# A mixture-of-experts stage on one core: expert loads in a fixed order, the last splits in twos behind y, the low part of the tokens between the halves of the one-hot matrix

## The chip, the core and the metric

The kernel runs on one core of a Trainium2 chip. The core has a matrix engine (TensorE, PE in the rows; PEld is its weight load), VectorE (DVE), ScalarE (ACT), GpSimd (POOL) and SyncE (SP), which issues nearly all DMAs. The metric is the device time of one execution in microseconds, the median of the runs shown. A profile of one execution gives the trace from which all rows come.

## What is computed

Two blocks of a language model run one after the other on 256 tokens of width 1024, in float32. The first has two layers of windowed attention and a gated recurrence. The second has attention, a short convolution and, at its end, a mixture of experts. All of it stays as it is but for the last part:

```
h2 = rms_norm_2(x, ffn_norm_g)
x = x + hierarchical_moe(h2, ...)   # top-1 of 4 groups, top-2 of its 4 experts, gates normalised
#   per expert: hid = silu(h w_gate) * (h w_up) * combine;  out += hid w_down      (16 experts, 1024 -> 256 -> 1024)
h3 = rms_norm_2(x, ple_norm_g)
x = x + sigmoid(h3 w_pg) * (p w_ple)
```

## The kernel before, in words

Every instruction is written in a program order with a priority, and a list scheduler puts each engine's instructions into one fixed order when the kernel is built; on the chip each engine goes through its own list and waits on semaphores. `ahead(g, n)` shifts the priority, `tc.issue_after(x)` holds what is traced within it behind x on x's engine. Tiles of one tag share a number of buffers, and an instruction that needs a buffer waits for the one that frees it.

*Weights.* All weights lie in one tensor `w_all`, cut into units of 128 x 2048 float32 (1.05 MB). For most of the kernel `Stream.load` brings a unit into one of three `raw` buffers and `Stream.prepare` splits each half of it into a high and a low part: a cast on ACT (whi, L270) and a subtraction on DVE (wlo, L271), each into a tile of the pool `t4` (4 KB per partition, `g.nt4` = 24 of them). `mm3` (L363 to L365) then makes three matmuls for each product. The 48 expert units (`plain0` to `plain1`) are not split. `Stream.fetch(ahead)` loads them up to `ahead` units past the one in use: every fourth into a `raw` buffer, the others in two halves into t4 tiles (named `wx`). `refill` is called after each use and tops this up to 12 units; once all are issued, it begins on the last four units (tag "pg") and prepares as many halves as the tiles set free allow.

*Routing and gather.* `moe` handles the tokens as two tiles t of 128. `choose(t)` finds the experts on DVE and builds the one-hot matrix D (128 tokens x 16 experts x 64 places) in two halves (L1325). `parts(t)` then splits the normed tokens into hh (ACT, L1331) and hl (DVE, L1332), held behind the second half of D. `gather(i, k, t, j)` (L1390) multiplies tokens with D into places, for the experts 8i to 8i + 7, and copies the result into hs; i = 0 runs before the experts and i = 1 after the first pair's gate and up products. `to_slots` finds the largest count of tokens in an expert (cnt), puts the gates in the order of places (psc, L1416; cs) and transposes D into DT (L1426, L1427).

*Experts.* They go in eight pairs q. `gate_up(q, j)` (L1440, two units each), `product(q)` (silu on ACT L1447, product on DVE L1448), `turn(q)` (transposes L1454, hidT on ACT L1456), `down(q)` (L1467, two units) whose result y is split into yh (ACT) and yl (DVE) by `split_to` (L538), and `scatter(q, t)` (L1479), which adds y back to the tokens through DT into four accumulators. After the first pair stands `overflow` (L1519), a branch around code for experts with over 64 tokens; the instructions of its two sides can't be moved past it.

*End.* `ple_out` calls `finish(t, c)`, which for c = 0 scatters the last pair, and adds the accumulator to x (L1487). Then follow the norm weight (L1585), transposes (L1588), the split into h3, the squares for the norm, and the pg product in column halves with the tanh (L1610), the products (L1611, L1612) and the store (L1613).

The loop over the pairs, on which the order depends:

```
for q in range(NP):
    if q + 1 < NP: gate_up(q + 1, 0)
    turn(q)
    if q + 1 < NP: gate_up(q + 1, 1); product(q + 1)
    if q: scatter(q - 1, 0); scatter(q - 1, 1)
    down(q)
```

Of the kernel before, what the change touches and what calls it, by code (L numbers as in the profile page):

```python
# [9 lines left out]
F32 = mybir.dt.float32  # L10
# [169 lines left out]
class Stream:  # L180
    RAW = 3

    def __init__(self, g):
# [12 lines left out]
        self.pieces = {}  # L196

    def fetch(self, ahead):


        g = self.g
        while self.loaded < min(self.used + ahead, self.plain1):
            i = self.loaded
# [3 lines left out]
            if (i - self.plain0) % 4 == 0:  # L207
                t = g.wp.tile([128, 2080], F32, tag="raw", name="raw", bufs=3)
                g.nc.sync.dma_start(out=t[:, :w], in_=src)
                self.pieces[i] = t[:, :h], t[:, h:w]  # L210
            else:
# [3 lines left out]
            self.loaded += 1  # L215

    def plain(self, tag, n):
# [3 lines left out]
        self.fetch(1)  # L221
# [3 lines left out]
    def refill(self):  # L225

        self.fetch(12)
        k = self.used + 12 - self.plain1
        if self.loaded >= self.plain1 and k > 0:
# [3 lines left out]
            first = (self.plain1 - 12 - self.plain0) % 4  # L233
            raws = len([j for j in range(k) if (j + first) % 4 == 0])
            self.RAW = min(3, raws)
            self.prepare(min(2 * self.plain1 + k - raws, 2 * self.plain1 + 2 * raws))
# [989 lines left out]
def moe(g, last):  # L1226
# [49 lines left out]
    for t in range(2):  # L1276
# [3 lines left out]
        D.append(small(f"D{t}", (NE, CAP), F32R))  # L1280
# [15 lines left out]
    def choose(t):  # L1296
# [18 lines left out]
        nc.vector.scalar_tensor_tensor(sel[:, t], rank[:, t], 2.0, oh[:, t].unsqueeze(2).to_broadcast([128, 4, 4]),  # L1315
# [7 lines left out]
        for i in range(2):  # L1323
            e = slice(8 * i, 8 * i + 8)
            last = nc.vector.tensor_tensor(D[t][:, e], place[:, t, e].unsqueeze(2).to_broadcast([128, 8, CAP]),  # L1325
                                           g.c("iota").unsqueeze(1).to_broadcast([128, 8, CAP]), op=OP.is_equal)
        return last

    def parts(t, a, b):
        with tc.issue_after(a.ins), tc.issue_after(b.ins):  # L1330
            nc.scalar.activation(hh[t], xw[t], AF.Copy, scale=rs[t])  # L1331
            nc.vector.scalar_tensor_tensor(hl[t], xw[t], rs[t], hh[t].bitcast(F32), op0=OP.mult, op1=OP.subtract)  # L1332
# [26 lines left out]
    def end(t, moved):  # L1359
        rs.append(mr[t].end())  # L1360
        placed = choose(t)
        parts(t, moved, placed)
        combine(t)

    with ahead(g, -20):
# [8 lines left out]
        g.st.fetch(8)  # L1374
        end(1, begin(1, 1))
    fl.all()
    g.st.fetch(11)
# [24 lines left out]
    g.st.fetch(12)  # L1402

    cs = small("cs", (NP,))
    DT = small("DT", (NP, 256), F32R)

    def to_slots():
# [13 lines left out]
        for t in range(2):  # L1421
            for b in range(2):
                ps = g.sm.tile([128, 4, 128], F32, tag="s", name="DTp")
                for q in range(4):
                    o = (4 * b + q) * 128
                    nc.tensor.transpose(ps[:, q], slots[t][:, o:o + 128].bitcast(F32), g.c("ident"))  # L1426
                nc.scalar.copy(DT[:, 4 * b:4 * b + 4, t * 128:(t + 1) * 128], ps)  # L1427

# [3 lines left out]
    def gate_up(q, j):  # L1432
# [3 lines left out]
        for k in range(4):  # L1436
            kk = 4 * j + k
            for i in range(2):
                half, o = divmod(2 * q + i, 8)
                nc.tensor.matmul(hid[q][64 * i:64 * i + 64], hs[half][kk // 4][:, kk % 4, o * 64:(o + 1) * 64],  # L1440
                                 w[i][k // 2][:, k % 2], start=(kk == 0), stop=(kk == KT - 1), skip_group_check=True)
        g.st.refill()

# [14 lines left out]
    def down(q):  # L1458
# [3 lines left out]
        for c in range(2):  # L1462
# [6 lines left out]
            split_to(g, y[q][0][:, c2], y[q][1][:, c2], ps)  # L1469
        g.st.refill()  # L1470

    def scatter(q, t):
# [3 lines left out]
        for c in range(2):  # L1476
# [5 lines left out]
    def finish(t, c):  # L1482

        if c == 0:
            scatter(NP - 1, t)
# [4 lines left out]
    to_slots()  # L1490
    gate_up(0, 0)
    gate_up(0, 1)
    product(0)
    for k in range(KT):
        for t, j in ((0, 0), (0, 1), (1, 0), (1, 1)):
            gather(1, k, t, j)
    overflow(g, cnti, wb, rs, place, comb)
    g.wb = load_row(g, "wb", h["ple_norm_g_2"][0])
    for q in range(NP):
# [6 lines left out]
        if q:  # L1506
            for t in range(2):
# [65 lines left out]
def ple_out(g, out, finish):  # L1573
# [4 lines left out]
    for t in range(2):  # L1578
        ts = slice(t * 128, (t + 1) * 128)
        xw = t4(g, "xw3", shape=(128, DM))  # L1580
        with ahead(g, 100):
            for b in range(2):
# [6 lines left out]
                split_to(g, hT[0][:, 4 * b:4 * b + 4, ts], hT[1][:, 4 * b:4 * b + 4, ts], ps)  # L1589
# [59 lines left out]
```

## Time and profile before

| what | value |
|---|---|
| timed runs | 776.31 us median of 3 (773.83, 776.31, 778.20) |
| profiled execution | 773.34 us, span 771.5 us |
| PE busy | 751.2 us (97%) |
| DVE, ACT busy | 453.3 us (59%), 350.6 us (45%) |
| DMA | 153.31 MB, mean 199 GB/s |

The span runs from the first to the last instruction; the execution's own time holds a little more around it. Busy PE time is not PE at its peak, since matmuls overlap and their ends are modelled. The rows below give times from the start of the span. In rows of the timeline, a note in brackets is the idle time of the engine before the instruction, and what ended it.

### The profile page before, as it was taken

The page shows a single profiled execution, that of the slowest core. Times are in us where ns is not written, and L with a number is a line of the kernel's source. Part 1 is how long each engine was busy: PE and PEld are TensorE (multiplying, and loading weights), DVE is VectorE, ACT ScalarE, POOL GpSimd, SP SyncE. Part 2 cuts the span into 40 slices and gives each one's busy share as a digit, 9 for nine tenths or more (in the row PEclk, how much of TensorE's full clock was granted, in tenths as well). Part 3 has the DMA queues.
Part 4 walks back from the last instruction along what each step waited for, and adds up shares of the span by engine and source line. Part 5 has one row for each costly group of instructions (what it writes and reads, how often), then busy time and mean ns, then how long its engine had stood idle before and what let it go on. Part 6 is the DMA issues. An engine that isn't in the chain of part 4 may idle for free. (4 is left out here: it accounts for less than half of the span.)

```text
span 771.5 us, 11965 instructions
## 1 busy us (share of the span) xinstructions
PE 751.2 (97%) x4894; PEld 616.2 (80%) x4894; DVE 453.3 (59%) x731; ACT 350.6 (45%) x579; POOL 21.3 (3%) x33
## 2 busy tenths in 40 slices
PE   7999999999999999999999999999999999999787
PEld 5899899799789888979987889999998853333356
DVE  6687487757577836668588676955474421011472
ACT  6761345845466315656447566643533421010441
POOL 0000000000000001000001310000000000000000
PEclk9999999999999999999999999999999999999999
DMA  8873044375266403337535441566468469999801
GB/s 305 321 277 110 8 157 165 115 266 183 79 208 262 170 1 110 110 110 273 219 132 197 165 164 59 202 223 218 177 231 302 165 220 388 415 418 415 349 4 54
DMA packets 29883, 153.31 MB, mean 199 GB/s; under 512 B 4600, under 2 KB 5632, under 8 KB 16768
## 3 DMA queue, kind: packets, MB, share of 16 engines
q1 hardware_dynamic: 29680, 152.45, 53.1%
q8 instruction: 39, 0.64, 0.3%
q14 instruction: 20, 0.16, 0.1%
q10 hardware_dynamic: 144, 0.07, 0.0%
HBM read 151.45 MB, written 1.05 MB: 198 GB/s over the span
## 5 line engine op out<-in xcount | busy, mean ns | idle before, releaser
L271 DVE TENSOR_TENSOR wlo<-raw,whi 128x1024 fp32r<-128x1024 f32 (+1 forms) x182 | 217.3, 1221 | 75.6 <-ACT whi L270 72.7
L270 ACT CAST whi<-raw 128x1024 fp32r<-128x1024 f32 (+1 forms) x182 | 184.3, 1050 | 52.0 <-PE acc L364 29.9
L363 PE MATMUL acc<-hTh,whi 128*128 128x256 f32 x608 | 173.6, 286 | 0.0
L365 PE MATMUL acc<-hTh,wlo 128*128 128x256 f32 x608 | 171.9, 283 | 0.0
L364 PE MATMUL acc<-hTl,whi 128*128 128x256 f32 x608 | 171.7, 282 | 0.0
L365 PEld LDWEIGHTS acc<-hTh,wlo 128*128 128x128 f32 x608 | 114.7, 189 | 3.2 <-issue 3.2
L363 PEld LDWEIGHTS acc<-hTh,whi 128*128 128x128 f32 x608 | 114.6, 188 | 1.7 <-issue 1.2
L364 PEld LDWEIGHTS acc<-hTl,whi 128*128 128x128 f32 x608 | 114.7, 189 | 0.3 <-issue 0.2
L363 PE MATMUL acc<-whi,hTh 128*128 128x512 f32 (+2 forms) x224 | 84.9, 379 | 0.8 <-ACT whi L270 0.8
L364 PE MATMUL acc<-wlo,hTh 128*128 128x512 f32 (+2 forms) x224 | 84.0, 375 | 0.4 <-DVE wlo L271 0.4
L365 PE MATMUL acc<-whi,hTl 128*128 128x512 f32 (+2 forms) x224 | 83.8, 374 | 0.0
L1440 PE MATMUL au<-wx,hs 128*64 128x512 f32 x192 | 58.9, 597 | 0.0
L1448 DVE SCALAR_TENSOR_TENSOR hid<-hid,cs,au 128x256 f32<-128x256 f32 x8 | 3.8, 481 | 79.4 <-ACT hid L1447 79.4
L363 PEld LDWEIGHTS acc<-whi,hTh 128*128 128x128 f32 x224 | 42.2, 188 | 7.2 <-ACT whi L270 1.2
L364 PEld LDWEIGHTS acc<-wlo,hTh 128*128 128x128 f32 x224 | 42.2, 189 | 6.7 <-DVE wlo L271 0.7
L365 PEld LDWEIGHTS acc<-whi,hTl 128*128 128x128 f32 x224 | 42.2, 188 | 6.3
L363 PE MATMUL acc<-whi,mTh 128*128 128x512 f32 x96 | 38.7, 403 | 0.0
L364 PE MATMUL acc<-wlo,mTh 128*128 128x512 f32 x96 | 38.1, 396 | 0.0
L365 PE MATMUL acc<-whi,mTl 128*128 128x512 f32 x96 | 38.0, 396 | 0.0
L1467 PE MATMUL y<-wx,hidT 128*64 128x512 f32 x96 | 30.8, 598 | 0.5 <-ACT hidT L1456 0.5
L1440 PEld LDWEIGHTS au<-wx,hs 128*64 128x64 f32 x192 | 17.2, 137 | 16.5 <-issue 15.5
L1440 PE MATMUL au<-raw,hs 128*64 128x512 f32 x64 | 29.1, 597 | 0.4 <-ACTq L1519 0.4
(329 smaller groups left out, 1237.3 us busy)
## 6 DMA issues: line engine op xcount, KB each, us to landing
raw<-in_w_all_dram SPq DMA_DIRECT2D x100, 1024.0 KB, 4.9
wx<-in_w_all_dram SPq DMA_DIRECT2D x72, 512.0 KB, 11.1
raw<-in_w_all_dram SPq DMA_DIRECT2D x2, 1040.0 KB, 4.8
x<-in_x_dram SPq DMA_DIRECT2D x2, 512.0 KB, 4.9
wb<-in_norm_w_dram SPq DMA_DIRECT2D x2, 512.0 KB, 6.2
raw<-in_w_all_dram SPq DMA_DIRECT2D x2, 512.0 KB, 8.2
out_dram<-sig SPq DMA_DIRECT2D x3, 256.0 KB, 2.0
wb<-in_final_norm_w_dram SPq DMA_DIRECT2D x1, 512.0 KB, 7.9
```

What stands on the lines that cost most here:

```text
L270: a = g.nc.scalar.copy(hi[:, :w], raw)
L271: b = g.nc.vector.tensor_sub(lo[:, :w], raw, hi[:, :w].bitcast(F32))
L363: nc.tensor.matmul(out, ah, bh, start=first, stop=False)
L364: nc.tensor.matmul(out, ah, bl, start=False, stop=False)
L365: nc.tensor.matmul(out, al, bh, start=False, stop=last)
L1440: nc.tensor.matmul(hid[q][64 * i:64 * i + 64], hs[half][kk // 4][:, kk % 4, o * 64:(o + 1) * 64], w[i][k // 2][:, k % 2], start=(kk == 0), ...
L1448: nc.vector.scalar_tensor_tensor(a, a, cs[:, q:q + 1], ps[:, 256:512], op0=OP.mult, op1=OP.mult)
L1467: nc.tensor.matmul(ps[64 * i:64 * i + 64], hT[:, k, 64 * i:64 * i + 64], w[i][k][:, 0, c2], start=(k == 0), stop=(k == 1), skip_group_chec ...
```

## The change

Expert loads are no longer issued by a count ahead. `give(*kinds)` hands the stream a list of free places ("t4": two t4 tiles, "raw": a raw buffer, "t8": one 8 KB tile of the pool t8), and units are put into them in a fixed order; `queue` holds each load behind the one before it. Units 0 and 1 go into t8 places, after the others that are listed before them. Each place that a used unit frees is given again, but for t8. `nt4` is 27, and D moves from the pool of its own into two t4 tiles. The pg halves are prepared behind the split of the last y (`after`), with 2, 4 and 6 allowed after the last three pairs. The low part hl is made in two halves, each ahead of one half of D, and hh in two halves. `turn_slots(0)` comes ahead of the experts, and the rest of `to_slots` behind gate_up(0, 0); gather(1) now comes ahead of gate_up(0, 1). The second tile's scatter of pair 6 and the scatter of pair 7 go by column halves in `finish`.

```
-        g.nt4 = 24
+        g.nt4 = 27
...
+        self.issued, self.cap = None, 0
+        self.early = deque((self.plain0, self.plain0 + 1))
+        self.order = deque(range(self.plain0 + 2, self.plain1))
+        self.room, self.spare = deque(), {"raw": 0, "t4": 0}
...
+    def give(self, *kinds):
+        g = self.g
+        self.room.extend(kinds)
+        while self.room and (self.order or self.early):
+            kind = self.room.popleft()
+            i = (self.early if kind == "t8" else self.order).popleft()
...
+            if kind == "t4":
                 self.pieces[i] = [t4(g, "wx", F32, (128, 1040))[:, :h] for _ in range(2)]
                 for c, t in enumerate(self.pieces[i]):
-                    g.nc.sync.dma_start(out=t, in_=src[:, c * h:(c + 1) * h])
+                    self.queue(t, src[:, c * h:(c + 1) * h])
+            else:
+                if kind == "t8":
+                    t = t8(g, "wx8", F32, (128, 2048))
+                else:
+                    t = g.wp.tile([128, 2080], F32, tag="raw", name="raw", bufs=3)
+                self.queue(t[:, :w], src)
+                self.pieces[i] = t[:, :h], t[:, h:w]
+            self.kinds[i] = kind
...
+    def queue(self, out, src):
+        with self.g.tc.issue_after(self.issued.ins) if self.issued is not None else ExitStack():
+            self.issued = self.g.nc.sync.dma_start(out=out, in_=src)
...
     def refill(self):
-        self.fetch(12)
-        k = self.used + 12 - self.plain1
-        if self.loaded >= self.plain1 and k > 0:
+        done = [i for i in sorted(self.kinds) if i < self.used]
+        self.give(*(k for k in map(self.kinds.pop, done) if k != "t8"))
+        if self.loaded >= self.plain1:
...
+            while self.room:
+                self.spare[self.room.popleft()] += 1
+            self.RAW = min(3, self.spare["raw"])
+            self.load(self.plain1 + self.RAW)
+            if self.behind:
+                self.prepare(2 * self.plain1 + min(self.spare["t4"], 2 * self.spare["raw"], self.cap))
...
-        D.append(small(f"D{t}", (NE, CAP), F32R))
+        D.append(t4(g, f"D{t}", F32R, (128, NE, CAP)))
...
+            c = slice(512 * i, 512 * i + 512)
+            with tc.issue_after(chosen.ins):
+                lo = nc.vector.scalar_tensor_tensor(hl[t][:, c], xw[t][:, c], rs[t], hh[t][:, c].bitcast(F32),
+                                                    op0=OP.mult, op1=OP.subtract)
+            with tc.issue_after(lo.ins):
+                chosen = nc.vector.tensor_tensor(D[t][:, e], place[:, t, e].unsqueeze(2).to_broadcast([128, 8, CAP]),
...
-        g.st.fetch(8)
+        g.st.give("t4", "t4", "raw", "t4", "t4", "raw", "t4", "t4", "t8")
         end(1, begin(1, 1))
     fl.all()
-    g.st.fetch(11)
+    g.st.give("t8", "t4", "t4", "raw", "t4")
...
+            last = split_to(g, y[q][0][:, c2], y[q][1][:, c2], ps)
+        if q > NP - 4:
+            g.st.after(*last)
+            g.st.cap = (2, 4, 6)[q - NP + 3]
         g.st.refill()
...
     def finish(t, c):
-        if c == 0:
-            scatter(NP - 1, t)
+        if t:
+            scatter(NP - 2, t, (c,))
+        scatter(NP - 1, t, (c,))
...
-    to_slots()
-    gate_up(0, 0)
-    gate_up(0, 1)
-    product(0)
+    turn_slots(0)
+    with tc.issue_after(gate_up(0, 0).ins):
+        to_slots()
     for k in range(KT):
         for t, j in ((0, 0), (0, 1), (1, 0), (1, 1)):
             gather(1, k, t, j)
+    gate_up(0, 1)
+    product(0)
     overflow(g, cnti, wb, rs, place, comb)
+    g.st.give("t4", "t4")
```

In `ple_out` the casts of pg are also held behind the split of the last h3 of each tile.

## Rows read from the trace of the kernel before

**Rows 1.** The page: busy time of PE; DMA share in 40 slices, in tenths.

```profile
PE 751.2 (97%) x4894; PEld 616.2 (80%) x4894; DVE 453.3 (59%) x731; ACT 350.6 (45%) x579; POOL 21.3 (3%) x33
...
DMA  8873044375266403337535441566468469999801
```

**Rows 2.** Stretches: length, busy time (instructions) of each engine, granted PE clock, DMA share, GB/s.

```profile
609.50:619.00 9.50, 9.50 (x36) 7.12 (x37) 3.59 (x6) 2.56 (x5) 0.00 (x0) 0.82 0.19 62
...
640.00:720.00 80.00, 80.00 (x358) 29.40 (x356) 9.88 (x17) 9.96 (x23) 0.00 (x0) 1.00 1.02 417
721.80:725.90 4.10, 0.00 (x0) 0.00 (x0) 0.47 (x1) 1.54 (x3) 0.00 (x0) 1.00 1.01 424
725.90:743.00 17.10, 14.57 (x46) 6.48 (x46) 13.55 (x17) 10.10 (x15) 0.00 (x0) 0.90 0.26 95
743.00:767.00 24.00, 23.95 (x132) 20.34 (x132) 11.92 (x22) 6.57 (x15) 1.38 (x2) 1.00 0.10 39
```

**Rows 3.** Timeline of PE, 720 to 745: start, length, instruction.

```profile
725.94 1.71 PE L1479 MATMUL acc<-yh,DT 128*128 128x512 f32 x3 [4.15 <-ACT yh L538]
...
730.58 1.07 PE L1467 MATMUL y<-wx,hidT 128*64 128x512 f32 x2 [0.46 <-ACT hidT L1456]
...
743.05 0.50 PE L363 MATMUL acc<-whi,h3h 128*128 128x512 f32 x1 [0.74 <-ACT h3h L538]
```

**Rows 4.** Timeline of ACT, 700 to 745.

```profile
714.86 0.37 ACT L1456 COPY hidT<-hTp 128x256 f32<-128x256 f32 x1 [8.10 <-PE hTp L1454]
718.40 0.38 ACT L1447 ACTIVATE hid<-au 128x256 f32<-128x256 f32 x1 [3.17 <-PE au L1440]
724.36 1.04 ACT L270 CAST whi<-raw 128x1024 fp32r<-128x1024 f32 x1 [5.57 <-DMA raw<-in_w_all_dram]
725.31 1.07 ACT L538 CAST yh<-y 128x512 fp32r<-128x512 f32 x2
726.26 2.95 ACT L270 CAST whi<-raw 128x1024 fp32r<-128x1024 f32 x3
730.15 0.37 ACT L1456 COPY hidT<-hTp 128x256 f32<-128x256 f32 x1 [0.94 <-PE hTp L1454]
...
735.94 0.58 ACT L538 CAST yh<-y 128x512 fp32r<-128x512 f32 x1 [2.55 <-PE y L1467]
```

**Rows 5.** Timeline of DVE, 700 to 745.

```profile
732.48 2.36 DVE L271 TENSOR_TENSOR wlo<-raw,whi 128x1024 fp32r<-128x1024 f32 x2
...
738.80 1.28 DVE L1487 TENSOR_TENSOR x<-x,acc 128x512 f32<-128x512 f32 x2 [1.55 <-PE acc L1479]
740.00 0.68 DVE L1585 TENSOR_TENSOR xw<-x,wb 128x512 f32<-128x512 f32 x1
```

**Rows 6.** The chain that ended last: start, length, what.

```profile
711.92 12.41 DMA raw<-in_w_all_dram
...
745.03 0.44 PE tr L1588 x4
```

**Rows 7.** Waits of SP, 560 to 771: line, releaser, us in total, times, longest.

```profile
SPq L214 <- DVE hl L1332: 12.5, 2, 7.2
...
SPq L1519 <- SPq L1519: 8.3, 7, 2.0
```

**Rows 8.** Timeline of SP, 626.8 to 637.

```profile
626.43 0.41 SPq L214 DMA_DIRECT2D wx<-in_w_all_dram  x1
635.41 0.34 SPq L594 DMA_DIRECT2D wb<-in_ple_norm_g_dram  x1
```

**Rows 9.** Timeline of PE, 602.5 to 634.5.

```profile
606.22 3.44 PE L1416 MATMUL psc<-comb,D 128*128 128x2 f32 x30
609.52 1.49 PE L1390 MATMUL acc<-D,hh 128*128 128x512 f32 x4
```

**Rows 10.** Timeline of DVE, 602.5 to 612.

```profile
610.07 1.28 DVE L1332 SCALAR_TENSOR_TENSOR hl<-xw,rs,hh 128x1024 fp32r<-128x1024 f32 x1
```

**Rows 11.** Timeline of ACT, 602.5 to 612.

```profile
606.91 2.07 ACT L1258 ACTIVATE ple<-acc 128x512 f32<-128x512 f32 x4
```

More of the change, by code (lines that the diff above doesn't have):

```diff
@@ L195, in __init__ @@
         self.used, self.limit = self.plain0, 2 * self.plain0
-        self.pieces = {}
-    def fetch(self, ahead):
+        self.pieces, self.kinds = {}, {}
+        self.issued, self.cap = None, 0
[3 more added lines that the diff above has]
+    def give(self, *kinds):
         g = self.g
-        while self.loaded < min(self.used + ahead, self.plain1):
-            i = self.loaded
+        self.room.extend(kinds)
+        while self.room and (self.order or self.early):
+            kind = self.room.popleft()
+            i = (self.early if kind == "t8" else self.order).popleft()
             tag, off, w = g.units[i]
@@ L206, in fetch @@
             h = w // 2
[L207 to L211, printed above, removed]
+            if kind == "t4":
                 self.pieces[i] = [t4(g, "wx", F32, (128, 1040))[:, :h] for _ in range(2)]
                 for c, t in enumerate(self.pieces[i]):
-                    g.nc.sync.dma_start(out=t, in_=src[:, c * h:(c + 1) * h])
-            self.loaded += 1
+                    self.queue(t, src[:, c * h:(c + 1) * h])
[7 more added lines that the diff above has]
+            self.kinds[i] = kind
+        if not self.order:
+            self.loaded = max(self.loaded, self.plain1)
+    def queue(self, out, src):
+        with self.g.tc.issue_after(self.issued.ins) if self.issued is not None else ExitStack():
+            self.issued = self.g.nc.sync.dma_start(out=out, in_=src)
     def plain(self, tag, n):
@@ L220, in plain @@
         assert self.g.units[i][0] == tag
-        self.fetch(1)
         self.used += 1
@@ L232, in refill @@
                 self.limit, self.bufs = self.n, 8
[L233 to L236, printed above, removed]
+            while self.room:
[4 more added lines that the diff above has]
+                self.prepare(2 * self.plain1 + min(self.spare["t4"], 2 * self.spare["raw"], self.cap))
     def after(self, *ins):
@@ L1324, in choose @@
             e = slice(8 * i, 8 * i + 8)
[L1325 to L1332, printed above, removed]
+            c = slice(512 * i, 512 * i + 512)
[4 more added lines that the diff above has]
+                chosen = nc.vector.tensor_tensor(D[t][:, e], place[:, t, e].unsqueeze(2).to_broadcast([128, 8, CAP]),
+                                                 g.c("iota").unsqueeze(1).to_broadcast([128, 8, CAP]), op=OP.is_equal)
     def combine(t):
@@ L1360, in end @@
         rs.append(mr[t].end())
-        placed = choose(t)
-        parts(t, moved, placed)
+        with tc.issue_after(moved.ins):
+            for c in range(2):
+                c2 = slice(c * 512, c * 512 + 512)
+                nc.scalar.activation(hh[t][:, c2], xw[t][:, c2], AF.Copy, scale=rs[t])
+        choose(t)
         combine(t)
@@ L1401, in moe, with turn_slots @@
             gather(0, k, t, j)
-    g.st.fetch(12)
     cs = small("cs", (NP,))
     DT = small("DT", (NP, 256), F32R)
+    def turn_slots(t):
+        for b in range(2):
+            ps = g.sm.tile([128, 4, 128], F32, tag="s", name="DTp")
+            for q in range(4):
+                o = (4 * b + q) * 128
+                nc.tensor.transpose(ps[:, q], slots[t][:, o:o + 128].bitcast(F32), g.c("ident"))
+            nc.scalar.copy(DT[:, 4 * b:4 * b + 4, t * 128:(t + 1) * 128], ps)
     def to_slots():
@@ L1420, in to_slots @@
             nc.vector.tensor_copy(cs[r], psc[r, :, i])
[L1421 to L1427, printed above, removed]
+        turn_slots(1)
     acc, hid, y = [], {}, {}
@@ L1439, in gate_up @@
                 half, o = divmod(2 * q + i, 8)
-                nc.tensor.matmul(hid[q][64 * i:64 * i + 64], hs[half][kk // 4][:, kk % 4, o * 64:(o + 1) * 64],
+                last = nc.tensor.matmul(hid[q][64 * i:64 * i + 64], hs[half][kk // 4][:, kk % 4, o * 64:(o + 1) * 64],
                                  w[i][k // 2][:, k % 2], start=(kk == 0), stop=(kk == KT - 1), skip_group_check=True)
         g.st.refill()
+        return last
     def product(q):
@@ L1468, in down, with scatter @@
                                      start=(k == 0), stop=(k == 1), skip_group_check=True)
-            split_to(g, y[q][0][:, c2], y[q][1][:, c2], ps)
+            last = split_to(g, y[q][0][:, c2], y[q][1][:, c2], ps)
+        if q > NP - 4:
+            g.st.after(*last)
+            g.st.cap = (2, 4, 6)[q - NP + 3]
         g.st.refill()
-    def scatter(q, t):
+    def scatter(q, t, cs=(0, 1)):
         if not acc:
@@ L1475, in scatter @@
         ts = slice(t * 128, (t + 1) * 128)
-        for c in range(2):
+        for c in cs:
             c2 = slice(c * 512, (c + 1) * 512)
@@ L1506, in moe @@
         if q:
-            for t in range(2):
+            for t in range(2 if q < NP - 1 else 1):
                 scatter(q - 1, t)
@@ L1588, in ple_out @@
                     nc.tensor.transpose(ps[:, k], xw[:, (4 * b + k) * 128:(4 * b + k + 1) * 128], g.c("ident"))
-                split_to(g, hT[0][:, 4 * b:4 * b + 4, ts], hT[1][:, 4 * b:4 * b + 4, ts], ps)
+                last = split_to(g, hT[0][:, 4 * b:4 * b + 4, ts], hT[1][:, 4 * b:4 * b + 4, ts], ps)
+            g.st.after(*last)
             mr = MeanRoot(g, g.x[t], xw, 4.0)
```

2 lines of the change are left out of this document (1 added, 1 removed).

## The prediction

> **What bounds the kernel now.** Four views, in this order. The page first: TensorE (PE) is busy for 97% of the span and the DMA slices are full only from the 34th of 40 on [rows 1]. That share is an average, so next the table by stretches [rows 2]. From 640 to 720 us PE starts 358 matmuls in 80 us, one per 0.223 us without a gap, while the DMA engines move 417 GB/s at a share of 1.02: both are full, and neither waits for the other. Then 721.8:725.9 has no matmul at all, and 725.9:743 has 46 in 17.1 us, which at 0.223 us each is 10.3 us of work. 743:767 has 132 matmuls in 24 us and is full again. So the one place with time to win late in the kernel is 721.8 to 743.05, where the first matmul of the gate's projection (tag "pg") starts [rows 3]: 21.3 us that hold 10.3 us of work, 11.0 us at most.
>
> Third, the order on ScalarE (ACT) says why PE stops [rows 4]. After the silu of pair 7 at 718.40, ACT stands for 5.57 us and the DMA of `raw` ends that wait: the cast of the first pg half (whi, L270) was put ahead of the eviction of pair 5's y (yh, L538, two at 725.31). That y had been complete for long; PE waits for yh 4.15 us [rows 3]. Three more casts then stand ahead of hidT of pair 7 (730.15), without which the last down product can't begin; it begins at 730.58. Its first half is evicted only at 735.94. Fourth, the chain: that first pg load was issued at 711.92 and took 12.41 us, to 724.33 [rows 6]. The loads are on the path through this one cast, not through the expert matmuls.
>
> **The change, part by part.**
>
> *Casts behind y.* `after` ties the casts of pg behind the split of the y just made, and `cap` lets 2, 4 and 6 halves through after pairs 5, 6 and 7. So whi 0 can't stand ahead of yh of pair 5 any more. Step 1: yh of pair 5 goes at 718.40 + 0.38 = 718.8 and is done by 719.9 (two take 1.07); its eight scatter matmuls (8 x 0.23 = 1.9 us) fill what is the gap at 721.8. Step 2: ACT then still stands before whi 0 until the load lands, since nothing ties the first two casts behind hidT of pair 7. With the load at 724.33 and two casts at about 1.0 us each (three end in 2.95 now, half counted for each of two halves of a unit), hidT comes at 726.4 in place of 730.15: 3.7 us. Step 3: from that start the first pg matmul is now 743.05 - 730.58 = 12.5 us away. Afterwards: first y half and four scatter matmuls, 12 x 0.25 = 3.0 us; two casts that may stand before the next eviction, 2.0; yh 0.58, yl 0.7 (taken as long as the norm weight), one matmul 0.23, the addition to x 0.64 (two in 1.28), the norm weight 0.68, four transposes 0.44, the split into h3 0.58 (as yh) [rows 4 to 6]: 8.9, less 0.7 us in which casts and y overlap (an estimate: the first cast can run while y's last matmuls do) = 8.2. That is 4.3 us less, because `finish` now needs only its own column half and scatter(6, 1) comes after the first half of the chain. Together -8.0. Bounds: step 2 alone, -3.7; the whole idle time, -11.0.
>
> *What is late next.* Pg units 2 and 3 and their casts. Each half costs VectorE (DVE) 1.2 us (two in 2.36) beside about 0.7 for each addition, norm weight and split [rows 5]; DVE is busy 13.55 of 17.1 us already [rows 2], and four of eight halves now fall into 735 to 745. PE reaches the fifth half one accumulation (24 x 0.23 = 5.6 us) after its start. I take +1.0 of waiting, between 0 and 3.6 (three halves not covered).
>
> *Loads in a fixed order, 14 units ahead in place of 12.* `nt4` goes from 24 to 27 tiles of 4 KB per partition, the two one-hot matrices D take two of them and two t8 tiles hold units 0 and 1. A unit is 1.05 MB, 2.5 us at 417 GB/s. More units ahead don't speed up PE, which never waits for them up to 721.8. They could bring the end of the stream forward. But SP doesn't issue past the branch around the overflow code: it waits there for the landing of everything in flight, 8.3 us [rows 7], so that nothing is issued between 626.43 and 635.41 [rows 8]. By then 16 units are issued (12 and 4 refills); afterwards too (14, and 2 refills after the second gate_up of pair 0, since t8 units give nothing back), and units 16 and 17 wait behind the branch together with the norm row. So the end of the stream hangs on when SP leaves the branch, R. From 635.41 to the first pg landing at 724.33 is 88.9 us for 33 units and the 0.5 MB row (35.1 MB, 84.2 us at the full rate); the landing is R + 88.9. R comes after gather(1) and gate_up(0, 1), but with two units in flight and not four: earliest when gather(1) frees hh, hl and D near 627.5, plus 4.5 us to land; latest after gate_up at 632 plus 5. That is 632 to 637, the landing 721 to 726. I take no change, with -3 to +2 in the range.
>
> *Low part between the halves of D.* Now hl of tile 1 stands last on DVE at 610.07 [rows 10]. Split in halves and put around the halves of D it would be done near 606, the same 1.28 us of work. PE begins gather(0) at 609.52, right after 30 psc matmuls of two columns [rows 9], and four ple evictions hold the accumulators until 609.0 [rows 11]. With psc and half of the transposes tied behind gate_up(0, 0), gather(0) can begin up to 3 us earlier, but the same 4.9 us of small matmuls come later, so only idle time and clock count. In 609.5:619 the granted clock was 0.82 [rows 2], a part of the time at 1.2 GHz in place of 2.4 after those small matmuls: 9.5 x 0.18 = 1.7 us that the other order may win or pay elsewhere. If the ple evictions stay late and nothing fills in, PE stands up to 3 us. I take -1.0, from -2.4 to +3.
>
> The Trainium skill, "TensorE: Matmul & The Clock Gate", section "HAM oscillation", says that idle gaps of PE throw it back to the slower of its clocks. The trace agrees: 725.9:743 has a granted clock of 0.90 right after the 4.1 us without a matmul, 1.7 us lost [rows 2]. By the rule the sum would be 1.7 us lower if the gap closes; by the row alone it lies within the 11.0 us.
>
> *Free edits.* scatter in column halves, turn_slots as a function and `queue` issue the same instructions. Two more tiles per unit in halves cost SP 0.33 us each, hidden while the stream is full.
>
> **Sum.** -8.0 + 1.0 - 1.0 + 0 = -8.0 us on the span of 771.5. Around the span lie 1.8 us (773.34 in all), so 765.3 for that execution. It was below all but the lowest of the timed runs (773.83 to 778.2, median 776.31); from the median the sum gives 768.3. I say 767.
>
> **The rivals.** (a) *The whole gap closes*: the stream ends 3 us earlier, hidT of pair 7 comes before the first cast, the clock stays up. -11 to -13, about 763. For it: eviction and hidT need no pg data. Against: on ACT the first cast has only yh ahead of it. 0.15. (b) *Loads late*: R near 637 or more, for the DMA engines stand idle once 14 units are in (share 0.19 in 609.5:619 even now, [rows 2]) and nothing comes back for t8 units. The first cast and hidT come 2 to 5 us later: 771 to 774. 0.15. (c) *It doesn't do what it says*: the first cast blocks hidT of pair 7, or of pair 6 (714.86 now, [rows 4]), as it blocked yh. Blocked from 714.86 until 726.4, pair 6's down product slips 11.6 us and eats the 8 to 11: 776. The Trainium skill, "Perfetto Trace Analysis", section "Identifying the Most-Contended Engine", would have the busiest engine improved first, which is PE, and nothing of PE's work goes; it warns in the same place that PE's busy share is a poor measure, and rows 2 show the gap. 0.08. (d) *Slower: units 0 and 1 stand ninth and tenth in a fixed line.* Any load that waits for a tile now holds all behind it. SP's longest wait for a tile ends with hl (7.2 us, [rows 7]), at 611.4. If unit 8 or 9 waits so long, unit 1 lands near 617 or later, gate_up(0, 0) can't start near 612, and psc can't fill in, being tied behind it. Gate_up(0, 0) begins at 618.9 now with psc done; 4.9 us of small matmuls later, each us after 614 is a us of PE; from a landing at 622 on the 8 us are gone, and at 628 the time is 782. Against it: three more tiles, and units 2 to 9 with unit 0 take 12 of the 27. 0.12. The forecast keeps 0.50.
>
> **Range and chances.** The forecast's own range is 762 to 772 (-13 to -4 from the median with its bounds). To hold 8 in 10, (a), (b) and half of (c) are taken in: 759 to 776. What two medians of three here can tell from no change is about 0.5%, 3.9 us. Faster by more: the forecast, (a) and half of (b), 0.73; within: half of (b) and (c), 0.15; slower: (d), 0.12.
>
> **What would show it.** Right: yh of pair 5 directly behind the silu of pair 7 with no DMA wait ahead of it; no 4 us gap on PE before scatter; the first pg matmul near 735; the granted clock at 1.0 in that stretch; D and hl halves alternating on DVE before 607. Wrong: ACT standing before a whi with hidT behind it; a first pg landing after 726; PE waiting for a DMA in the expert loop or before gate_up(0, 0); gaps between pg accumulations with wlo as the releaser, longer than 3.6 us together. The prediction falls if the time saved before 743 comes back behind the pg start, or if the order of the first 560 us shifts with the larger pool, which I take as nothing since PE is full there.

## The result, and the profile after

The changed kernel takes 785.18 us (median of 4 runs, 783.98 to 785.89) beside 775.77 us for the kernel before (4 runs, 773.83 to 778.20): the ratio is 1.0118, 95% interval 1.0086 to 1.0151. It is slower by about 9 us, where 767 and a range of 759 to 776 were forecast. The profiled execution took 785.89 us, its span 784.1 us (before 771.5).

The page: busy time of PE, and the DMA share in 40 slices.

```profile
PE 757.3 (97%) x4894; PEld 620.4 (79%) x4894; DVE 451.9 (58%) x733; ACT 350.3 (45%) x581; POOL 21.8 (3%) x33
...
DMA  8872134455257204427642632764479339999601
```

PE makes the same 4894 matmuls as before and its share is still 97% [rows 1]; in the 33rd slice (627 to 647 us) DMA stands at 3 tenths, where the 33rd of before (617 to 636) had 6. The stretches tell more (columns as in rows 2; the edges are moved with the work):

```profile
619.00:640.00 21.00, 19.02 (x91) 14.56 (x91) 3.81 (x9) 5.19 (x8) 0.00 (x0) 0.84 0.23 72
640.00:720.00 80.00, 79.98 (x360) 29.61 (x362) 10.69 (x18) 10.55 (x24) 0.00 (x0) 1.00 0.97 389
720.00:730.00 10.00, 9.51 (x42) 3.61 (x41) 0.48 (x1) 0.76 (x2) 0.00 (x0) 1.00 1.03 418
730.00:755.00 25.00, 14.88 (x41) 5.82 (x41) 13.37 (x17) 8.94 (x13) 0.00 (x0) 0.78 0.33 126
```

The expert loop from 640 to 720 runs as before. The hole before the pg product has grown: 730 to 755 holds 41 matmuls in 25 us, at a granted clock of 0.78, where 725.9 to 743 held 46 in 17.1 [rows 2]. Timeline of ACT from 718 on:

```profile
723.56 0.38 ACT L1468 ACTIVATE hid<-au 128x256 f32<-128x256 f32 x1 [3.17 <-PE au L1460]
732.37 1.99 ACT L287 CAST whi<-raw 128x1024 fp32r<-128x1024 f32 x2 [8.42 <-DMA raw<-in_w_all_dram]
734.27 1.07 ACT L555 CAST yh<-y 128x512 fp32r<-128x512 f32 x2
735.22 0.38 ACT L1477 COPY hidT<-hTp 128x256 f32<-128x256 f32 x1
```

The same wait as in rows 4, only for other work: yh of pair 5 is out in time, but yh of pair 6 and hidT of pair 7 now stand behind the first two casts, and these wait 8.42 us for the load. The first cast starts 8.0 us later than before (724.36, [rows 4]). Timeline of PE in the same place:

```profile
734.90 0.79 PE L1503 MATMUL acc<-yh,DT 128*128 128x512 f32 x1 [5.39 <-ACT yh L555]
...
753.13 1.94 PE L1615 MATMUL tr<-const,xw 128*128 128x128 f32 x8 [3.77 <-DVE xw L1612]
754.90 0.79 PE L380 MATMUL acc<-whi,h3h 128*128 128x512 f32 x1
```

The gap that was to close is 5.39 us and not 4.15 [rows 3], and a second one of 3.77 us has come, with the norm weight (xw) as its releaser. Timeline of DVE ahead of it:

```profile
748.83 1.22 DVE L288 TENSOR_TENSOR wlo<-raw,whi 128x1024 fp32r<-128x1024 f32 x1 [0.26 <-ACT whi L287]
749.98 1.28 DVE L1512 TENSOR_TENSOR x<-x,acc 128x512 f32<-128x512 f32 x2
751.17 1.22 DVE L288 TENSOR_TENSOR wlo<-raw,whi 128x1024 fp32r<-128x1024 f32 x1
752.31 1.28 DVE L1612 TENSOR_TENSOR xw<-x,wb 128x512 f32<-128x512 f32 x2
```

Before, the first norm weight stood right behind the first two additions [rows 5]; now two low halves (cast 4 and 5) and the additions of the other token tile stand between them. The first pg matmul comes at 754.90, 11.85 us after the 743.05 of before [rows 3].

The loads: SP's timeline (600 to 634, 640 to 648, 715 to 735) and one row of its waits.

```profile
604.05 30.05 SPq L231 DMA_DIRECT2D wx<-in_w_all_dram  x4
...
643.06 1.79 SPq L231 DMA_DIRECT2D wx<-in_w_all_dram  x4
...
719.86 1.61 SPq L266 DMA_DIRECT2D raw<-in_w_all_dram  x2
```

```profile
SPq L231 <- PE acc L1409: 24.5, 2, 24.2
```

The row of four issues that is drawn out over 30 us hides a wait of 24.2 us: half a unit waits for a tile that is held until the end of gather(1), near 634. What is issued then has to land before SP leaves the branch: its first issue behind it is at 643.06, and not at 635.41 [rows 8]. The first pg load goes out at 719.86 in place of 711.92 [rows 6].

PE's front, timeline from 604 to 641:

```profile
606.47 1.96 PE L1409 MATMUL acc<-D,hh 128*128 128x512 f32 x4 [0.42 <-ACT ple L1275]
...
619.15 5.20 PE L1442 MATMUL psc<-comb,D 128*128 128x2 f32 x32
...
634.04 0.40 PE L1409 MATMUL acc<-D,hl 128*128 128x512 f32 x1
...
640.02 0.61 PE L1460 MATMUL au<-raw,hs 128*64 128x512 f32 x1 [1.99 <-DVEq L1546]
```

gather(0) starts 3 us earlier than in rows 9, as was hoped. But the last matmul of gather(1) starts only at 634.04, and gate_up(1, 0), behind the branch, at 640.02; before it started at 633.99.

About 2 us of these differences lie between the two executions and not in the change. Three more profiles with the front of before (those of the late load, of the casts alone and of the 766.57 us below) have gate_up(1, 0) at 635.86 to 636.08 and SP's first issue behind the branch at 637.14 to 637.71. From 600 to 640 their granted clock was 0.91, as in the profile of the changed kernel; in the profile of before it was 0.96. The two profiled spans lie 12.6 us apart, the medians 9.4.

### The profile page after: what moved, and what is told of

Its sections match the earlier page's. It is cut to its first block, busy times and chain, and to the rows that moved or that the text cites. A ratio compares the mean times of both kernels' runs of the same rounds, so it can differ in the third digit from the quotient of the medians.

```text
span 784.1 us, 11957 instructions
## 1 busy us (share of the span) xinstructions
PE 757.3 (97%) x4894; PEld 620.4 (79%) x4894; DVE 451.9 (58%) x733; ACT 350.3 (45%) x581; POOL 21.8 (3%) x33
## 5 line engine op out<-in xcount | busy, mean ns | idle before, releaser
L287 ACT CAST whi<-raw 128x1024 fp32r<-128x1024 f32 (+1 forms) x182 | 182.4, 1050 | 35.5 <-DMA raw<-in_w_all_dram 34.3
L922 PEld LDWEIGHTS sc<-QA,FK 128*128 128x128 f32 x192 | 27.6, 191 | 1.8 <-DVE QA L928 0.5
```

The costliest lines, as they stand in the source:

```text
L287: a = g.nc.scalar.copy(hi[:, :w], raw)
L922: nc.tensor.matmul(ps[:, 4 * t + a], K[:, a, ts], q2t[:, a], start=True, stop=True)
```

## The experiments

Each run had its own runs of the kernel before on the same chip (medians 774.4 to 775.4 us). Ratios are to these, with 95% intervals; below 1 is faster.

### Late loads, and casts that stand ahead of others

**The kernel before with a late pg load:** the first pg unit is loaded twice.

```
...
+                if self.loaded == self.plain1:
+                    g.nc.sync.dma_start(out=t[:, :w], in_=src)
                 g.nc.sync.dma_start(out=t[:, :w], in_=src)
...
```

> The kernel before, with the first pg unit loaded twice into its buffer, so that its last copy lands later and nothing else is changed. Theory L (late loads: the end hangs on the landing of the first pg unit, because ScalarE stands before its cast with y and hidT of the last pairs behind it): the cast of the first half moves from 724.4 to 731 or later, and the first pg matmul and the end move by at least two thirds of that, 5 us or more. Theory P (TensorE's own order at the front sets the time): the landing doesn't matter by itself, the end moves by under 2 us.

Measured 780.91 us, 1.0081 (1.0064 to 1.0098). The first cast on ACT and the scatter on PE:

```profile
731.82 1.04 ACT L272 CAST whi<-raw 128x1024 fp32r<-128x1024 f32 x1 [10.98 <-DMA raw<-in_w_all_dram]
```

```profile
733.40 1.71 PE L1481 MATMUL acc<-yh,DT 128*128 128x512 f32 x3 [9.56 <-ACT yh L540]
```

The first cast comes 7.5 us later than in the profile of before (2 us of it from the later front in this execution), and the first pg matmul with it, 7.7 us later (750.79). The medians differ by 6.5 us (780.91 less 774.40). While a cast stands ahead of the chain, the delay of the load passes to the end.

**gate_up(0, 1) first:** the changed kernel with the order of the kernel before in one place.

```
+    gate_up(0, 1)
+    product(0)
     for k in range(KT):
         for t, j in ((0, 0), (0, 1), (1, 0), (1, 1)):
             gather(1, k, t, j)
-    gate_up(0, 1)
-    product(0)
```

> The changed kernel with gate_up(0, 1) and product(0) put back ahead of gather(1), nothing else. Theory L: the refills that gate_up(0, 1) sets free are issued near 625 and not 634, they have landed when SP stands at the branch, SP goes on near 630 to 633 in place of 643, the first pg cast comes at 722 to 725 in place of 732.4, and the time falls by 5 to 9 us to 776 to 780. Theory P: TensorE's work up to the branch is the same, only its stand of 2 us at the branch may go, so 783 to 785. Theory T (the new order at the end is the cost): 785, whatever the loads do.

Measured 779.07 us, 1.0058 (1.0041 to 1.0075): 0.6% of the 1.2% come from this order. SP and ACT:

```profile
629.27 11.52 SPq L231 DMA_DIRECT2D wx<-in_w_all_dram  x7
```

```profile
727.46 2.00 ACT L287 CAST whi<-raw 128x1024 fp32r<-128x1024 f32 x2 [3.38 <-DMA raw<-in_w_all_dram]
...
730.32 0.38 ACT L1477 COPY hidT<-hTp 128x256 f32<-128x256 f32 x1
```

The held halves go out at 629.27 in place of 633.78, SP's first issue behind the branch is at 638.38 in place of 643.06, and the first cast comes 4.9 us earlier. hidT of pair 7 still stands behind it.

**The casts alone:** the kernel before with `after` and the caps 2, 4, 6 behind y, and behind h3, as in the change.

> The kernel before with one part of the change alone: pg halves held behind the last y, 2, 4 and 6 of them, and behind h3. Loads, one-hot matrix, gather and scatter stay as before. Its order on ScalarE has hidT of pair 7 ahead of the first two casts, and y of pair 6 behind them. Theory L: with the load landing near 724 the y of pair 5 and hidT of pair 7 go before it, the 4 us gap goes, and the time falls by 4 to 8 us, to 768 to 772. Theory T: the casts behind y are themselves the cost, since they come later: no gain or a loss, 775 to 782.

Measured 773.32 us, 0.9983 (0.9973 to 0.9993): less than was expected of this part. hidT of pair 7 and yh are in time (727.40, ahead of the first cast) and the 4 us gap is gone, but PE waits before the transposes:

```profile
741.18 1.97 PE L1593 MATMUL tr<-const,xw 128*128 128x128 f32 x8 [4.62 <-DVE xw L1590]
```

```profile
735.77 2.48 DVE L1492 TENSOR_TENSOR x<-x,acc 128x512 f32<-128x512 f32 x4
738.17 2.35 DVE L273 TENSOR_TENSOR wlo<-raw,whi 128x1024 fp32r<-128x1024 f32 x2
740.43 1.29 DVE L1590 TENSOR_TENSOR xw<-x,wb 128x512 f32<-128x512 f32 x2
```

The gain is given back on DVE: with six casts let through by y, the low halves of cast 4 and 5 go ahead of the norm weight.

**Casts behind hidT:** the changed kernel, with no pg cast until hidT of pair 7 and the y of pair 6 are out; then 4, and 6 behind the last y.

```
...
-        nc.scalar.copy(hid[q], ps)
+        ins = nc.scalar.copy(hid[q], ps)
+        if q == NP - 1:
+            g.st.after(*hid["y"], ins)
+            g.st.cap = 4
+            g.st.refill()
...
```

> The changed kernel with no pg cast allowed until hidT of pair 7 and y of pair 6 are issued on ScalarE (four casts behind them, then six behind y of pair 7); the loads are late as in the changed kernel. If ScalarE's stand before the first cast with y of pair 6 and hidT of pair 7 behind it is what the late landing costs (theory L), TensorE's gap of 5.4 us at 729.5 goes, and the time falls by 4 to 8 us, to 777 to 781, though the loads are as late as before. If the late landing costs through the pg matmuls themselves or the cost is elsewhere (P, T), 783 to 786.

Measured 777.17 us, 1.0035 (1.0021 to 1.0049), 6.4 us below the changed kernel by the ratios (8.0 by the medians), with loads as late as there:

```profile
729.72 0.38 ACT L1477 COPY hidT<-hTp 128x256 f32<-128x256 f32 x1
732.07 1.99 ACT L287 CAST whi<-raw 128x1024 fp32r<-128x1024 f32 x2 [1.97 <-DMA raw<-in_w_all_dram]
```

A late load costs little once nothing stands behind its cast. The gap of 4.71 us before the transposes is still there.

### Front order, DVE's order, and the parts together

**Slot counts first:** the changed kernel with `to_slots()` whole ahead of `gate_up(0, 0)`, without the tie.

> The changed kernel with to_slots whole ahead of gate_up(0, 0), so that the fetch of slot counts, the four remaining transposes and their copies no longer stand between gate_up(0, 0) and gather(1). If the front order on TensorE costs the time by itself (theory P: small matmuls at the lower clock behind gate_up, gate_up(1, 0) at 640.0 and not 634.0), gate_up(1, 0) begins 2 to 5 us earlier, the last loads before the branch are issued as much earlier, and the time is 779 to 783. If it is only the loads held by the tile owners (gather(1) still ahead of gate_up(0, 1)), the loads move by no more than gather(1)'s own end and the time is 783 to 786.

Measured 784.02 us, 1.0109 (1.0080 to 1.0138). gate_up(1, 0) starts at 639.85, as in the changed kernel (640.02). The small matmuls come to lie between gather(0) and gate_up(0, 0) and take as long there; theory P, as it was put, fails.

**Caps 2, 4, 4:** casts 4 and 5 behind h3 and not behind y of pair 7.

```
-            g.st.cap = (2, 4, 6)[q - NP + 3]
+            g.st.cap = (2, 4, 4)[q - NP + 3]
```

> The changed kernel with a cap of 2, 4, 4: casts 4 and 5 of pg go behind the first split of h3 and not behind y of pair 7. Theory T (the end of the chain is late because VectorE makes two low halves and four additions ahead of the first norm weight): the 3.77 us gap ahead of the first tr falls to about 1.5, the first pg matmul comes 2 to 3 us earlier and the time is 782 to 783.5. If the casts on ScalarE or the loads alone set it (theory L), the first pg matmul stays within 0.5 us of 754.9 and the time at 785.

Measured 779.02 us, 1.0063 (1.0038 to 1.0087). The gap before the transposes is gone altogether:

```profile
745.78 0.68 DVE L1612 TENSOR_TENSOR xw<-x,wb 128x512 f32<-128x512 f32 x1
746.42 0.69 DVE L555 TENSOR_TENSOR yl<-y,yh 128x512 fp32r<-128x512 f32 x1
```

```profile
747.01 0.60 PE L1615 MATMUL tr<-const,xw 128*128 128x128 f32 x4
747.37 0.71 PE L1503 MATMUL acc<-yl,DT 128*128 128x512 f32 x2
748.29 0.50 PE L380 MATMUL acc<-whi,h3h 128*128 128x512 f32 x1 [0.20 <-ACT h3h L555]
```

That is 4.3 us by the ratios (6.2 by the medians) for one number in the source, more than the 1.7 to 3.2 us that theory T asked for. The front is 1.4 us earlier in this profile (gate_up(1, 0) at 638.60), and the lower clock behind the gap went with the gap: 753 to 757.7 had 0.51 granted in the changed kernel and 1.00 here.

**Both repairs:** the changed kernel with gate_up(0, 1) first, four casts behind hidT of pair 7, the others behind h3.

> The changed kernel with three repairs at once: gate_up(0, 1) and product(0) ahead of gather(1) (loads about 4.5 us earlier, as in the run that did this alone), no pg cast until hidT of pair 7 and the y of pair 6 are out, then four, and the others behind h3. If late loads, the casts ahead of hidT and the new order on VectorE are the whole loss (theories L and T), the parts add up: 785.2 - 6 - 8 + 3 (shared) - 2 = 772, range 769 to 775. If something else of the change costs (the one-hot matrices in larger tiles, the tied queue, the low part in halves), it stays at 776 or more.

Measured 771.79 us, 0.9960 (0.9945 to 0.9975), as the sum said.

**The kernel before with these casts:** its own loads and front, casts as in the run above.

> The kernel before, with its own loads and its own front, and the casts ordered as in the run beside it: none until hidT of pair 7 and the y of pair 6 are out, then four, the others behind h3. Casts behind y alone, with 2, 4 and 6 halves, gave 0.998 because two low halves stood ahead of the norm weight on VectorE. Theory T: without those two the 4.6 us gap ahead of tr falls to about 2, the first pg matmul comes at 739 to 741 and the time is 768 to 771. If the casts only move the wait from one place to another (no gain to be had while DMA sets the landing), 773 to 775.

Measured 766.57 us, 0.9892 (0.9867 to 0.9917): the fastest of all. ACT and PE:

```profile
727.23 0.38 ACT L1458 COPY hidT<-hTp 128x256 f32<-128x256 f32 x1
727.50 3.90 ACT L272 CAST whi<-raw 128x1024 fp32r<-128x1024 f32 x4
```

```profile
736.46 1.17 PE L1595 MATMUL tr<-const,xw 128*128 128x128 f32 x8 [1.24 <-DVE xw L1592]
737.76 0.50 PE L365 MATMUL acc<-whi,h3h 128*128 128x512 f32 x1
```

No DMA ends a wait of ACT here, and from gate_up(1, 0) at 635.86 to the first pg matmul are 101.9 us; before it was 743.05 - 633.99 = 109.1.

### The loads, the gather order, and the rest of the front

**Loads of before in the changed kernel:** 12 units ahead, no t8 tiles, gate_up(0, 1) first; then the same with the casts behind hidT.

```
-        g.st.give("t4", "t4", "raw", "t4", "t4", "raw", "t4", "t4", "t8")
+        g.st.give("raw", "t4", "t4", "t4", "raw", "t4", "t4", "t4")
...
-    g.st.give("t8", "t4", "t4", "raw", "t4")
+    g.st.give("raw", "t4", "t4", "t4")
...
```

> The changed kernel with the loads of before (12 units ahead, no t8 tiles, units in their own order) and gate_up(0, 1) ahead of gather(1); its casts (2, 4, 6 behind y), its one-hot matrices and its split low part stay. If the loads are the larger part of the loss (theory L), SyncE leaves the branch at 635 to 636.5, the first pg unit lands at 724 to 726 and the time is 772 to 776, as the casts alone gave. If the tiles are innocent and the front of the changed kernel (theory P) holds SyncE at the branch anyway, it leaves at 638 and the time is 778 to 780, as with gate_up first alone.

> The same with the casts as in the version of the kernel before that reached 766.6: none until hidT of pair 7 and the y of pair 6 are out, then four, the others behind h3. What is left of the change in it is the order of the front (low part between the halves of the one-hot matrix, slot counts behind gate_up(0, 0)) and the additions in halves. If these are worth the 1.0 us that was forecast, 765 to 766; if the longer stretch of small matmuls in the front costs what it shows in the trace, 768 to 770.

Measured 777.11 us, 1.0026 (1.0016 to 1.0036), and 771.91 us, 0.9975 (0.9957 to 0.9992). ACT in the first:

```profile
731.21 0.37 ACT L1477 COPY hidT<-hTp 128x256 f32<-128x256 f32 x1 [5.54 <-PE hTp L1475]
731.48 1.99 ACT L287 CAST whi<-raw 128x1024 fp32r<-128x1024 f32 x2
```

Neither theory of the first has all of it. No cast waits for the DMA, but SP's first issue behind the branch comes at 639.70: it waits there for DVE for 2.7 us, since PE's front is as late as in the change. Beside the run with gate_up(0, 1) first, from which only the loads differ, it is faster by 0.0032 (2.5 us, the intervals lie apart). There ACT's list has the first two casts ahead of hidT of pair 7, here behind it, as in the run of the casts alone. So with the casts of the change the new loads cost time by the place that the scheduler then gives the casts, and not by a later branch. With the casts behind hidT this is gone: the second run is no faster than with 14 units in the order of the change (771.79). Its 771.91 is more than either theory of it allowed: beside 766.57 there are 5 us left for the rest of the change.

**Low part in halves alone**, and **gather(1) ahead of gate_up(0, 1) alone**, both in the version of 766.57.

> The version of the kernel before that reached 766.6 (casts behind hidT of pair 7), with one more part of the change and no other: the low part in halves between the halves of the one-hot matrix, hh in halves. If that step was worth the 1.0 us of the forecast, 765 to 766. If it is what moved the small matmuls behind gather(0) and made gather(0) meet the evictions of ple (theory P: front 4 to 5 us longer in the runs that have the change's front), gate_up(1, 0) begins 2 to 5 us later than in that run and the time is 768 to 771.

> The same version of the kernel before, with only gather(1) put ahead of gate_up(0, 1) and product(0), loads 12 ahead as they are there. Theory O (the order of TensorE before the branch holds the last loads, whatever the tiles): SyncE leaves the branch 4 to 8 us later than 637, the first pg unit lands as much later, ScalarE waits for it ahead of the first whi and the time is 771 to 776. If it takes the tied order of loads and the t8 tiles as well, 766 to 768.

The low part: 767.50 us, 0.9891 (0.9866 to 0.9915). gate_up(1, 0) starts 0.8 us later; no gain, no loss. The gather order: 770.89 us, 0.9938 (0.9917 to 0.9958), about 4 us lost with the loads of before. PE and SP show both halves of it:

```profile
637.68 0.61 PE L1442 MATMUL au<-raw,hs 128*64 128x512 f32 x1 [1.97 <-DVEq L1526]
```

```profile
640.58 0.34 SPq L596 DMA_DIRECT2D wb<-in_ple_norm_g_dram  x1
```

PE stands 1.97 us at the branch where it stood 0.47, since product(0) is now the last work of ACT and DVE ahead of it; and SP leaves it 3.4 us later than the 637.14 of the version it was put into, because refills wait for gather(1). With casts this tolerant, that costs ACT only 0.7 us of waits for DMA.

**Slot counts late**, and **the largest count early again**, in the version with the low part in halves.

> The version of before that reached 767.5 (casts behind hidT of pair 7, low part in halves), with one more part of the change: the slot counts, psc and half of the transposes tied behind gate_up(0, 0). If this is what makes the changed front longer (theory F1), gate_up(1, 0) begins at 639 to 640 and not 636.7, the branch stand grows from 0.4 to 1.5 and the time is 770 to 772. If the rest of the change does it (the tied queue, tiles, additions in halves, theory F2), 767 to 768.

> The same, but the largest count (four psp matmuls, the reduction and cnti) made ahead of gate_up(0, 0) and only psc and the transposes behind it. If the branch stands longer because the count is made late and VectorE reads it behind its last hs copy, the stand falls back to 0.4 to 0.5 and the time is 1 us below the run beside it. If the place of the read in VectorE's list doesn't hang on it, the stand and the time stay as in the run beside it.

768.81 us, 0.9918 (0.9901 to 0.9935), and 768.48 us, 0.9906 (0.9885 to 0.9928). The branch stand is 0.40 in both; F1 falls for the most part, and the late count isn't what makes the branch longer.

**The tie taken away** from the 771.91 version (each load issued with no `issue_after`), and **additions in halves** added to the 768.81 version (`scatter(q, t, cs)` and `finish` as in the change).

> The version of the changed kernel that gave 771.9 (loads of before, casts behind hidT of pair 7), with the expert loads no longer tied one behind another on SyncE. Theory Q: the tie is what lengthens its front beside the 768.8 of the run with the slot counts late (by the later start of the branch in every engine's list); then 769 and a branch stand of 0.4. If the tie is harmless, 771.5 to 772 and a stand of 1.5.

> The version of before that gave 768.8 (casts behind hidT of pair 7, low part in halves, slot counts late), with the last part of the change: the last two pairs scattered in column halves and the additions to x behind their own half. If the column halves are worth what the forecast's step 3 drew from them, 766 to 768; if they cost, 770 to 772.

Without the tie 771.07 us, 0.9957 (0.9944 to 0.9971); the branch stand falls from 1.54 to 0.40, and the time by less than the two intervals can tell apart. So the tie is a second cause of the longer stand at the branch. The halves cost: 771.24 us, 0.9959 (0.9946 to 0.9973), 0.4% above 0.9918 (3.2 us by the ratios, 2.4 by the medians). The same 34 matmuls of the last pair, first with halves, then without (stretches, columns as in rows 2):

```profile
727.30:736.80 9.50, 9.41 (x34) 3.93 (x33) 7.37 (x9) 5.76 (x8) 0.00 (x0) 1.00 0.61 222
```

```profile
727.20:735.70 8.50, 8.39 (x34) 3.63 (x33) 7.38 (x9) 5.69 (x8) 0.00 (x0) 1.00 0.73 247
```

In the timeline of the first, single scatter matmuls stand between pairs of y matmuls (128 x 64 each, two at a time):

```profile
728.54 1.07 PE L1478 MATMUL y<-wx,hidT 128*64 128x512 f32 x2
729.55 0.49 PE L1491 MATMUL acc<-yl,DT 128*128 128x512 f32 x1
729.97 1.07 PE L1478 MATMUL y<-wx,hidT 128*64 128x512 f32 x2
730.97 0.49 PE L1491 MATMUL acc<-yl,DT 128*128 128x512 f32 x1
```

Without halves the 16 y matmuls stand in one block:

```profile
729.39 3.65 PE L1478 MATMUL y<-wx,hidT 128*64 128x512 f32 x16
```

A pair takes 0.45 us in the block (3.59 us to the next scatter matmul, at 732.98, for eight pairs) and 1.0 us when it stands alone between scatter matmuls. The two profiled spans differ by 1.2 us, about this; the rest of the difference between the medians is not seen in the profiles.

### The steps in one table

Ratio to the kernel before; 0.001 is 0.78 us. Each row takes one thing out of the row above, but for the one that names two. The steps in us are worked out from the ratios.

| version | ratio | step |
|---|---|---|
| the changed kernel | 1.0118 | |
| gate_up(0, 1) ahead of gather(1) | 1.0058 | -4.7 us |
| four casts behind hidT of pair 7, others behind h3 | 0.9960 | -7.6 us |
| loads of before | 0.9975 | none that shows |
| loads not tied | 0.9957 | none that shows |
| additions whole (and tiles of before) | 0.9918 | -3.0 us |
| slot counts in their old place | 0.9891 | -2.1 us, intervals overlap |
| low part whole | 0.9892 | 0 |

## Why the prediction was wrong

**"Loads in a fixed order" is the first step that failed.** It took R, the moment when SP leaves the branch, as 632 to 637 and the landing as 721 to 726, "no change". R was 643 and the cast started at 732.37, 8.0 us later than in the profile of before; beside the other profiles with the front of before, R is 5.4 to 5.9 us later. The step saw that R hangs on gather(1) and on what is in flight, but it let gather(1) end near 627.5; it ended at 634.4, because another part of the same change had put 7.1 us of small matmuls ahead of it (618.68 to 625.82). And it took 4.5 us for two units to land; from the issue at 633.78 to the first issue behind the branch it was 9.3. The rule R + 88.9 held: 643.06 + 88.9 = 732.0, and with gate_up(0, 1) first 638.38 + 88.9 = 727.3, where the cast started at 727.46. Rival (b) had late loads by 2 to 5 us, but from idle DMA engines. That a load which waits for a tile holds all behind it is rival (d), which looked for it ahead of gate_up(0, 0); this began at 615.10, in place of 618.89, and the held load was another. For R the gather order is the cause: with it put back R falls by 4.7 us, and put into the other version alone it costs 3.4; with the loads of before R doesn't fall (639.70). The new loads do harm elsewhere: with them the first two casts come ahead of hidT of pair 7 in ACT's list.

**"Casts behind y", steps 1 to 3.** Step 1 was right: yh of pair 5 goes first. Step 2 said that nothing ties the first two casts behind hidT of pair 7, and gave hidT 726.4 for a load at 724.33; the mechanism was right, and with the load at 732.37 it gave hidT 735.22, a loss of 5.1 us where a gain of 3.7 stood. With the same casts and the loads of before, hidT stands ahead of the casts (727.40 and 731.21, two runs), so it takes both parts of the change to make this block. yh of pair 6 was held too, which no step had. Rival (c) named this block, and priced it at a gain just eaten up. Step 3 made the chain from hidT to the first pg matmul 4.3 us shorter; it became 6.8 us longer (754.90 - 735.22 = 19.7, before 12.9). It counted two casts on ACT ahead of yh, and took the norm weight to follow the first addition. It did not list what DVE would do between, which the caps decide: two more additions and two low halves, 3.7 us (1.28 and twice 1.22). The column halves, on which the step drew, cost 1.0 us of PE.

**"What is late next"** put the pressure on DVE at +1.0, behind the pg start (pg units 2 and 3). DVE was the place, but the wait came ahead of the start, 3.77 us and the lower clock behind it.

**"Low part between the halves of D"**, -1.0 with a bound of +3: gate_up(1, 0) came 6.0 us later. About 2 us of this is the clock of the front in the two executions. The low part itself is worth nothing that shows either way (0.9891 and 0.9892). The order around it costs: gather(1) ahead of gate_up(0, 1), which lengthens the stand at the branch (0.47 to 1.97 us in the run that did this alone), and the tie of the loads (0.40 to 1.54). What the late slot counts cost is not clear of the intervals.

**"Free edits"** priced the column halves at nothing because they issue the same instructions. They do, and cost 2.4 us in their run by the medians (3.2 by the ratios), of which the profiles show 1.2: the order of matmuls of two shapes is no free edit.

**The clock.** 735 to 742 had 0.60 granted after the gap of 5.39 us, 753 to 757.7 had 0.51 after the gap of 3.77 us: a part of the time at 1.2 GHz in place of 2.4. The Trainium skill, "TensorE: Matmul & The Clock Gate", section "HAM oscillation", has idle gaps throw PE back to the slower clock; these two places agree.

Casts that hold up nothing, with the load in time, give 766.57 (0.9892), beside a forecast of 767. That the two meet is luck: 4.3 of the forecast's 8.0 us were drawn from a shorter chain with column halves, and that version has no column halves. The errors of the sum were to take the load as unmoved, though step 2 let hidT hang on it, and to leave out what the caps put on DVE ahead of the norm weight. A small one in its last line: the profiled 773.34 was below all three timed runs, not all but the lowest.

What stays open: the 2.1 us of the slot counts' place are within what two intervals can tell; why the granted clock of the front differs between executions of the same code; and whether the tie or the tiles hold a part of the 3.0 us of the halves was not told apart further.

## What to carry to other kernels

A tie behind one instruction protects that instruction alone: list everything that the engine still has to do for the chain before the held work may go, on the second engine that the held work feeds too, and tie behind the last of these. When an edit moves work ahead of a branch or a buffer's last reader, follow the queue that stands in order behind it, for the transfer that it holds back may be needed 90 us later. Price the parts of a change together where one sets the time that another takes as given.

## What the hardware showed that was not expected

The granted clock fell in the front with no gap on PE: from 618.7 to 626 PE was busy for 7.30 of 7.30 us, with 47 matmuls, nearly all of 2 to 128 columns, and 0.66 was granted; 32 psc matmuls took 5.20 us. In the run with the count early the same 32 took 3.7 us at a granted clock of 1.00 (619 to 625), between the same gate_up and transposes, so this order makes the fall possible, not certain.

Interleaving matmuls of 128 x 64 (two at a time) with single ones of 128 x 128 cost 1.0 us over 34 matmuls, at a granted clock of 1.00 and with 0.1 us idle in either order.
